# A two-layer hybrid encoder: another order of the instructions, ten weight tiles made by DMA, squares on ScalarE, an output stage in two halves

## The chip, the cores and the metric

The kernel runs on one core of a Trainium2 chip. The metric is the device time of one execution in microseconds (us), the median of several runs. A profiled execution gives the trace from which the rows below come. Engines: PE is TensorE, PEld its weight loads, DVE is VectorE, ACT is ScalarE, POOL is GpSimd, SP is SyncE, which here issues DMAs only.

## What is computed

The reference is an encoder trunk of two layers on 512 tokens of width 1024, all in float32. Per layer:

```python
h = rms_norm(x, g_mix);  z = h @ w_in            # 1024 -> 2560: q, k, v, xb, gb
o = diff_attention(rope(q), rope(k), v, lam)     # 4 heads, two score maps of width 64 each
c = centred_dwconv(xb)                           # width 4
h_f, h_b = rg_lru(c, forward), rg_lru(c, reverse)
r = rms_norm((h_f + h_b) * gelu(gb), lru_norm_g)
x = x + concat(rms_norm(o), r) @ w_out
x = x + cross_attention(rms_norm(x), rms_norm(mem))   # 4 heads, 256 memory tokens
x = x + square(relu(rms_norm(x, g_mlp) @ mlp_w1)) @ mlp_w2   # 4096 hidden
```

and after both layers `rms_norm(x, g_final)`.

## The kernel before

The residual stream lies transposed in SBUF as eight tiles `x[c]` of 128 channels by 512 tokens. Each float32 operand of a large matmul is used as two float32r parts: `hi`, the value as ScalarE converts it on writing a float32r tile, and `lo`, the difference, which VectorE subtracts (`split`). A product is three matmuls: hi by hi, hi by lo and lo by hi, added up in PSUM. The weights lie in memory as 126 tiles of 128 by 1024 a layer. `weight` loads one with a DMA on SP into a `wraw` tile (three buffers), and splits it into `whi` and `wlo` (three buffers each); `gemm_fm` makes from it 24 matmuls of 128x128 by 512 columns. The second MLP product works on pairs of weight tiles: `right_pair` and `left_pair` form sums and differences, and `seven` computes a 2x2 block product by seven half-wide products in place of eight, each of 12 matmuls of 256 columns, and adds them to halves (`LO`, `HI`) of two residual tiles. In `mlp_pair`, a tile of the first MLP product is multiplied by the broadcast norm `rb` and put through max(t, 0) * t, both on VectorE.

A layer has these stages: the v products, a mixing stage (16 units of attention, `FILL` microseconds of other work placed after each, which a generator takes from the letters of `ORDER`: X, Y convolutions, P, R gates, p, r scans, 1 to 3 heads, B and b the gate branch, N its norm, K the keys and values of the memory), the output projection, cross-attention, its projection, and the MLP in four blocks.

The program is first recorded as a list of operations. `Plan.schedule` then places them: each engine takes, of the operations that can begin soonest, the one with the smallest key. A key is the TensorE time recorded before the operation, less a lead in us (`plan.ahead`): `LOAD_AHEAD` for loads, `SPLIT_AHEAD` for splits, `ATT_AHEAD` for attention. `cost` prices each operation, and buffers are counted. A ScalarE operation that needs another function table has `SWITCH` added to its key, and `WAIT` to its start if it would begin late. The resulting order is emitted as the order of each engine's queue; each queue is in order on the chip. All operations are emitted by one line, L414, so a row is told apart by its tile names.

A norm collects squares (`Norm.add`), sums over partitions by matmuls with a column of ones, scales on VectorE, takes the power -1/2 on GpSimd (`rsqrt_small`), and is broadcast by TensorE transposes (`bcast`). At the end eight outputs of 128 by 512 are multiplied with the last broadcast, two on GpSimd and six on VectorE, and stored by SP.

Of the kernel before, what the change touches and what calls it, by code (L numbers as in the profile page):

```python
# [11 lines left out]
F32 = mybir.dt.float32  # L12
# [28 lines left out]
NW = 3  # L41
NSM = 24
NMM = 3
ORDER = ["XYPp1Rr2B3bNK", "XY1Pp2Rr3BbNK"]
FILL = [[8.6, 7.6, 8.6, 7.6, 10.8, 9.7, 11.9, 6.5, 11.9, 7.6, 8.6, 10.8, 7.6, 5.4, 5.4, 7.6],
        [10.8, 7.6, 8.6, 7.6, 8.6, 10.8, 6.5, 10.8, 10.8, 10.8, 7.6, 7.6, 9.7, 3.2, 1.1, 6.5]]
LAG = 2
POOL_OUT = (0, 1)
ATT_AHEAD = 3
SPLIT_AHEAD = 12.0  # L50
LOAD_AHEAD = 65.0


PC = {}
# [96 lines left out]
class Plan:  # L151
# [5 lines left out]
    OWN = {"pe": 0.0, "dve": 0.127, "act": 0.1, "pool": 0.1, "sp": 0.05}  # L157
    LOOK = 0.0
    TABLE = 1.283
    SWITCH = 25.0  # L160
    WAIT = 2.5
    SETS = {"Exp": ("exp",), "Tanh": ("exp", "sig", "gelu"), "Sigmoid": ("sig",), "Sqrt": ("sqrt",),
            "Gelu_apprx_tanh": ("gelu",), "Sin": ("sin",)}

# [30 lines left out]
    def cost(self, eng, m, a, k):  # L195
        out = a[0] if a else k["out"]
        n = 1
        for d in out.shape[1:]:
            n *= d
        if eng == "pe":  # L200
            if m == "transpose":
                return 0.109
            f32 = a[1].root.dtype == F32
            if n < 64:
                return 0.224
            return n * 0.00176 if f32 else max(0.114, n * 0.000456)
        if m == "dma_start":
            return 0.06
        if eng == "act":
            t = 0.093 + n * 0.000833  # L210
            t += 0.093 * sum(isinstance(k.get(x), _View) for x in ("scale", "bias", "accum_out"))
            return t
        if eng == "dve":
            if m == "tensor_reduce":
                n = 512
            if m == "tensor_scalar_mul":
                return 0.066 + n * 0.0007
            ap = m == "scalar_tensor_tensor" and isinstance(a[2], _View)
            return 0.067 + n * 0.00105 + 0.06 * ap
        if eng == "pool" and n <= 4:  # L220
            return 1.0
        if eng == "pool":
            return 0.1 + n * (0.0022 if m != "memset" else 0.001)
        return 0.06

    def record(self, eng, m, a, k):
# [18 lines left out]
        if m == "dma_start":  # L245
            v = out[0] if out else k["in_"]
            op.bytes = 4
            for d in v.shape:
                op.bytes *= d
        if m == "activation":  # L250
            op.table = self.SETS.get(str(a[2]).split(".")[-1])
        for v in allv:
# [18 lines left out]

    def schedule(self):
        ops = self.ops
        for op in ops:
            op.preds.discard(op)
            op.behind -= op.preds | {op}
            op.npred = len(op.preds) + len(op.behind)
            for p in op.preds:
                p.succ[op] = True
            for p in op.behind:  # L280
                p.succ[op] = False
# [34 lines left out]
        def look(e):  # L316
            best, smin, tries = [], 1e18, 0
            for key, idx in cand[e]:
                op = ops[idx]
                st = max(free_at[e], op.ready)  # L320
                ok = True
                need = {}
                for r in op.new:
                    if r.tag in slots:
                        need[r.tag] = need.get(r.tag, 0) + 1
                for tag, n in need.items():
                    fr = sorted(slots[tag])[:n]
                    st = max(st, fr[-1])
                    w, h = waiting[tag], head[tag]
                    while h < len(w) and w[h] in placed:  # L330
                        h += 1
                    head[tag] = h
                    if st >= 1e17:
                        ok = False
                    elif w[h] != idx and n + sum(i > w[h] for i in alive[tag]) > spare[tag]:
                        ok = False
                tries += 1
                if ok:
                    if op.table and table not in op.table:
                        key += self.SWITCH  # L340
                        st += self.WAIT if st > free_at[e] else 0.0
                    best.append((st, key, idx))
                    smin = min(smin, st)
                if tries >= 60 and best:
                    break
            if not best:
                return None
            lim = smin + self.LOOK
            return min(((k, i, s) for s, k, i in best if s <= lim))

        dirty = set(self.engines)
        while left:
# [5 lines left out]
                raise RuntimeError("no instruction can be placed: " + str(  # L358
                    {t: sum(s < 1e17 for s in v) for t, v in slots.items()}))
            e = pick[1]  # L360
            _, idx, st = choice[e]
            op = ops[idx]
            cand[e].remove((op.key, idx))
            dur = op.dur
# [52 lines left out]
def trunk(tc, ctx, xT, memT, pos, W, par, outT):  # L417
# [18 lines left out]
    def T():  # L436
        return plan.tile("b", [P, S], F32)
# [24 lines left out]
    def raw_weight(l, t, ahead=None):  # L462
# [8 lines left out]
                SP.dma_start(out=raw, in_=W[l * NT + t])  # L471
        return raw

    def weight(l, t):
        raw = pre.pop(t, None) if l == 0 else None
        first = raw is not None
        if raw is None:
# [43 lines left out]
    def pc(l, name, i):  # L521
        o = l * NPL + PC[name] + i
        return prm[:, o:o + 1]

    ident = C([P, P], F32, "ident")
    G.memset(ident, 0.0)
# [470 lines left out]
        out[3] = [(dh[:, i * P:(i + 1) * P], dh[:, 512 + i * P:512 + (i + 1) * P]) for i in range(4)]  # L997
        return out

    def seven(l, ta, tb, left, ca, cb, order=range(4)):  # L1000

        w = right_pair(l, ta, tb)
        X, Y, Z = MM(), AT(), AT()
# [15 lines left out]
        add(ca, LO, X, ALU.add)  # L1019
        prod(2, Z, True)  # L1020
        add(ca, LO, Z, ALU.add)
        prod(6, X, False)
        add(cb, LO, X, ALU.subtract)
        prod(5, Y, True)
# [155 lines left out]
    def mlp_pair(l, bk, p, xs, rb):  # L1180

        ts = []
        for i in (2 * p, 2 * p + 1):
            pm = MM()
            gemm_fm(l, T_W1 + 8 * bk + i, xs, pm)
            t = T()
            V.tensor_tensor(t, pm, rb, op=ALU.mult)
            V.scalar_tensor_tensor(t, t, 0.0, t, op0=ALU.max, op1=ALU.mult)
            ts.append(t)
        return left_pair(*ts)  # L1190

# [21 lines left out]
    for l in range(DEPTH):  # L1213
# [64 lines left out]
        def finish(hd, h):  # L1278
# [3 lines left out]
                cat[h] = hd.out()  # L1282
            later(1, out)

        for u in range(16):
            h, qc = divmod(u, 4)
            if qc == 0:
# [50 lines left out]
        for bk in range(4):  # L1338
# [2 lines left out]
                nrm = Norm()  # L1341
                xs = [None] * KD
            for m in range(0, 8, 2):
                seven(l, T_W2 + 8 * bk + m, T_W2 + 8 * bk + m + 1, hid, m, m + 1)
                for c in (m, m + 1) if bk == 3 else ():
                    if l + 1 < DEPTH:
                        xs[c] = prep_x(l + 1, "g_mix", c, nrm)
                    else:
                        nrm.add(x[c])
                        xs[c] = T()  # L1350
                        A.activation(xs[c], x[c], AF.Copy, scale=prm[:, P_FINAL + c:P_FINAL + c + 1])
            if bk < 3:
                nxt += [mlp_pair(l, bk + 1, p, xs, rb) for p in range(1, 4)]
            hid = nxt

    rt = nrm.rstd(D, 4)
    bp = AT()
    bcast(rt, 4, bp)
    rb = plan.tile("rb", [P, S], F32)
    A.activation(rb, bp, AF.Copy)  # L1360
    for c in POOL_OUT + tuple(c for c in range(KD) if c not in POOL_OUT):
        o = T()
        if c in POOL_OUT:
            G.tensor_tensor(o, xs[c], rb, op=ALU.mult)
        else:
            V.tensor_tensor(o, xs[c], bp, op=ALU.mult)
        SP.dma_start(out=outT[c * P:(c + 1) * P, :], in_=o)

    order = plan.schedule()
    plan.emit(tc, order)  # L1370
# [73 lines left out]
```

## Time and profile before

| what | value |
|---|---|
| median of 3 runs | 1506.97 us (1505.68 to 1511.34) |
| the profiled execution's own time | 1508.43 us |
| its span, first to last instruction | 1506.6 us |
| mean granted TensorE clock | 0.984 |
| busy: TensorE, VectorE, ScalarE, GpSimd | 1446.8, 1159.3, 731.7, 26.5 us |
| TensorE matmul instructions | 8038 |
| DMA traffic | 152.43 MB, on average 101 GB/s |
| share of the chain of waits: TensorE, VectorE, ScalarE | 80%, 11%, 4% |

Matmuls are pipelined, and a matmul's busy time overlaps the next one's; so a busy share of TensorE near 100% means that it always had a matmul under way, and not that each took its shortest time. The granted clock of a stretch is a share of 2.4 GHz; a value between 0.5 and 1 is a mean over time at 1.2 and at 2.4 GHz.

### The profile page before, as it was taken

The page shows a single profiled execution, that of the slowest core. Times are in us where ns is not written, and L with a number is a line of the kernel's source. Part 1 is how long each engine was busy: PE and PEld are TensorE (multiplying, and loading weights), DVE is VectorE, ACT ScalarE, POOL GpSimd, SP SyncE. Part 2 cuts the span into 40 slices and gives each one's busy share as a digit, 9 for nine tenths or more (in the row PEclk, how much of TensorE's full clock was granted, in tenths as well). Part 3 has the DMA queues.
Part 4 walks back from the last instruction along what each step waited for, and adds up shares of the span by engine and source line. Part 5 has one row for each costly group of instructions (what it writes and reads, how often), then busy time and mean ns, then how long its engine had stood idle before and what let it go on. Part 6 is the DMA issues. An engine that isn't in the chain of part 4 may idle for free.

```text
span 1506.6 us, 20763 instructions
## 1 busy us (share of the span) xinstructions
PE 1446.8 (96%) x8038; PEld 1239.1 (82%) x8038; DVE 1159.3 (77%) x1959; ACT 731.7 (49%) x1105; POOL 26.5 (2%) x46
## 2 busy tenths in 40 slices
PE   8978999999999999999999989999999999999996
PEld 6756888888888989898887768888888898988985
DVE  7888886555679797887958799855556887969695
ACT  6587765334434343433534887643443433434343
POOL 1000000000000000000000000000000000000000
PEclk9988999999999999999999999999999999999998
DMA  5332442321222222222224444432122223232321
GB/s 198 112 101 71 144 153 92 112 70 43 99 97 93 104 99 98 98 96 101 85 103 121 112 106 149 137 112 83 59 70 84 99 99 112 82 104 89 118 84 58
DMA packets 47666, 152.43 MB, mean 101 GB/s; under 512 B 6096, under 2 KB 6224, under 8 KB 47568
## 3 DMA queue, kind: packets, MB, share of 16 engines
q1 hardware_dynamic: 47424, 150.85, 30.2%
q8 instruction: 63, 1.03, 0.3%
q14 instruction: 35, 0.29, 0.1%
q10 hardware_dynamic: 144, 0.26, 0.1%
HBM read 136.41 MB, written 2.10 MB: 92 GB/s over the span
## 4 chain that ended last, share of the span: by engine, by line
PE 80%; DVE 11%; ACT 4%; issue 2%; DMA 1%; SPq 1%; POOL 0%; DVEq 0%; ACTq 0%; POOLq 0%
PE mm L414 63%; PE at L414 18%; DVE b L414 6%; DVE wlo L414 3%; ACT b L414 3%; DVE pt L414 1%; ACT L414 1%; SPq L414 1%; DMA b<-b 1%; DVE s L414 1%; ACT whi L414 0%; POOL s L414 0%; DVE c_x L414 0%; DMA wraw<-in_memT 0%; DMA c_x<-in_xT 0%
## 5 line engine op out<-in xcount | busy, mean ns | idle before, releaser
L414 PE MATMUL mm<-b,whi 128*128 128x512 f32 (+1 forms) x3648 | 985.5, 358 | 11.7 <-ACT b L414 5.0
L414 PEld LDWEIGHTS mm<-b,whi 128*128 128x128 f32 x3648 | 638.5, 189 | 119.7 <-ACT b L414 6.3
L414 PE MATMUL mm<-b,wlo 128*128 128x512 f32 (+1 forms) x1824 | 650.1, 356 | 10.2 <-DVE wlo L414 10.2
L414 ACT ACTIVATE whi<-wraw 128x1024 fp32r<-128x1024 f32 (+1 forms) x223 | 233.4, 1048 | 357.4 <-issue 155.2
L414 PEld LDWEIGHTS mm<-b,wlo 128*128 128x128 f32 x1824 | 344.5, 189 | 67.4 <-DVE wlo L414 12.6
L414 DVE TENSOR_TENSOR wlo<-wraw,whi 128x1024 fp32r<-128x1024 f32 (+1 forms) x223 | 268.9, 1206 | 40.9 <-ACT whi L414 40.4
L414 DVE TENSOR_TENSOR b<-b,b 128x512 fp32r<-128x512 f32 (+2 forms) x390 | 224.7, 593 | 16.0 <-ACT b L414 14.4
L414 ACT ACTIVATE b<-b 128x256 fp32r<-128x256 f32 (+2 forms) x224 | 130.3, 596 | 150.2 <-DVE b L414 146.7
L414 DVE TENSOR_TENSOR c_x<-c_x,mm 128x256 f32<-128x256 f32 (+1 forms) x160 | 73.7, 471 | 77.8 <-PE mm L414 76.4
L414 ACT ACTIVATE whi<-pt 128x1024 fp32r<-128x1024 f32 x64 | 67.9, 1061 | 101.8 <-PE mm L414 75.7
L414 PE MATMUL at<-b,whi 128*128 128x256 f32 x512 | 92.0, 278 | 0.0
L414 DVE TENSOR_TENSOR b<-mm,rb 128x512 f32<-128x512 f32 x72 | 49.4, 687 | 53.5 <-PE mm L414 53.4
L414 DVE TENSOR_TENSOR wlo<-pt,whi 128x1024 fp32r<-128x1024 f32 x64 | 78.1, 1220 | 0.6 <-ACT whi L414 0.3
L414 ACT ACTIVATE b<-at,s 128x512 f32<-128x512 f32 (+2 forms) x100 | 61.0, 617 | 34.8 <-DVE s L414 34.1
L414 PEld LDWEIGHTS at<-b,whi 128*128 128x128 f32 x512 | 77.7, 188 | 0.0
L414 PE MATMUL at<-b,b 128*128 128x256 f32 (+1 forms) x320 | 67.3, 341 | 5.8 <-DMA b<-b 3.7
L414 DVE TENSOR_REDUCE s<-at 128x1 f32<-128x512 f32 (+1 forms) x80 | 54.3, 686 | 24.0 <-PE at L414 24.0
L414 PE MATMUL at<-b,wlo 128*128 128x256 f32 x256 | 71.2, 278 | 0.0
L414 PEld LDWEIGHTS at<-b,b 128*128 128x128 f32 x320 | 48.2, 196 | 13.6 <-DMA b<-b 4.4
L414 PE MATMUL at<-pt,b 128*128 128x256 f32 (+1 forms) x288 | 51.3, 325 | 4.9 <-ACT pt L414 2.9
L414 DVE TENSOR_TENSOR c_x<-c_x,at 128x256 f32<-128x256 f32 x96 | 40.0, 417 | 18.4 <-PE at L414 17.8
L414 PEld LDWEIGHTS at<-pt,b 128*128 128x128 f32 x288 | 43.8, 192 | 11.5 <-ACT pt L414 3.2
(124 smaller groups left out, 1267.0 us busy)
## 6 DMA issues: line engine op xcount, KB each, us to landing
wraw<-in_W SPq DMA_DIRECT2D x249, 512.0 KB, 3.3
b<-b SPq DMA_DIRECT2D x96, 128.0 KB, 2.3
wraw<-in_memT SPq DMA_DIRECT2D x4, 512.0 KB, 4.3
out_T<-b SPq DMA_DIRECT2D x8, 256.0 KB, 2.6
c_x<-in_xT SPq DMA_DIRECT2D x7, 256.0 KB, 6.1
wraw<-in_W SPq DMA_DIRECT2D x6, 256.0 KB, 4.8
c_x<-in_xT ACTq DMA_DIRECT2D x1, 256.0 KB, 3.2
c_prm<-in_par SPq DMA_DIRECT2D x1, 89.0 KB, 3.0
```

The lines of the kernel that those rows point to most:

```text
L414: getattr(self.engines[op.eng], m)(*a, **k)
```

## The change

A table `LEADS` has one character for each recorded operation; it shifts that operation's key by between -20 and +20 us. The letter L stands for no shift; most operations have another. The mixing stages' `ORDER` and `FILL` are others; loads and splits get longer leads; the planner prices a DMA issue at 0.43 us (0.9 on GpSimd) instead of 0.06, and treats table switches and its sequence of starts a little differently.

Five weight tiles a layer (`DMA_T`: the keys of head 0, the queries of head 2, one tile of the gate branch, one of the memory keys, the last of the memory values) are no longer loaded raw. A GpSimd DMA converts the tile from memory into `whi`; ScalarE writes its negative into `wlo`; a second GpSimd DMA adds the tile from memory to that.

In `mlp_pair` one VectorE operation makes max(pm, 0) * rb, and ScalarE squares it. The last `seven` of the kernel runs its products in another order (`early`), in which three of the four residual halves are done before the last two products, and the last norm and the outputs are made for each half of the tokens by itself: sixteen stores of 128 by 256. There the squares of the last two residual tiles are added by the matmuls with ones instead of by VectorE, and the gain `g_final` is applied by the VectorE multiply, so that ScalarE's scaled copies remain for GpSimd's two tiles only.

```diff
-ORDER = ["XYPp1Rr2B3bNK", "XY1Pp2Rr3BbNK"]
-FILL = [[8.6, 7.6, 8.6, 7.6, 10.8, 9.7, 11.9, 6.5, 11.9, 7.6, 8.6, 10.8, 7.6, 5.4, 5.4, 7.6],
-        [10.8, 7.6, 8.6, 7.6, 8.6, 10.8, 6.5, 10.8, 10.8, 10.8, 7.6, 7.6, 9.7, 3.2, 1.1, 6.5]]
+ORDER = ["XYPp1Rr23BKbN", "XYP1p2Rr3BbNK"]
+FILL = [[14.1, 2.1, 8.6, 0.0, 17.3, 6.7, 6.9, 7.5, 11.9, 7.1, 0.0, 15.3, 13.2, 7.4, 4.4, 15.2],
+        [8.8, 14.6, 8.6, 9.6, 9.1, 7.4, 1.5, 15.3, 15.8, 16.8, 1.8, 1.1, 6.5, 1.5, 3.7, 4.0]]
+PRE = [0.0, 0]
-SPLIT_AHEAD = 12.0
-LOAD_AHEAD = 65.0
+SPLIT_AHEAD = 18.0
+LOAD_AHEAD = 105.0
+CAST_AHEAD = 28.0
+NEG_AHEAD = 20.0
+DMA_T = (1, 4, 13, 36, 51)
+LEAD_STEPS = '#$%&()*+,-./0123456789:;<=>?@ABCDEFGHIJKLMNOPQRSTUVWXYZ[]^_`abcdefghijklmnopqrstu'
+LEADS = (
+    'uL63BCuGGgGGGG@@<<HGuue>d>auFOMu9Q-ZAAGA-2D-H)?NNOC*@%AD?EA#6&/,0,?CBBB,=5>BBDFA?1J1C-G;JF$80?FUFKP;'
...
-    SWITCH = 25.0
-    WAIT = 2.5
+    SWITCH = 52.0
+    WAIT = 3.5
+    HOLD = 0.0
...
         if m == "dma_start":
-            return 0.06
+            return 0.9 if eng == "pool" else 0.43
...
+        for op, c in zip(ops, LEADS):
+            op.key -= LEAD_STEPS.index(c) / 2 - 20.0
...
+    def weight_dma(l, t):
+        hi = plan.tile("whi", [P, 1024], F32R)
+        lo = plan.tile("wlo", [P, 1024], F32R)
+        src = W[l * NT + t]
+        with plan.ahead(CAST_AHEAD):
+            G.dma_start(out=hi, in_=src)
+        with plan.ahead(NEG_AHEAD):
+            A.activation(lo, b(hi), AF.Copy, scale=-1.0)
+            G.dma_start(out=lo, in_=src, accum_op=ALU.add)
+        return hi, lo
+
     def weight(l, t):
+        if t in DMA_T:
+            return weight_dma(l, t)
...
-            V.tensor_tensor(t, pm, rb, op=ALU.mult)
-            V.scalar_tensor_tensor(t, t, 0.0, t, op0=ALU.max, op1=ALU.mult)
+            V.scalar_tensor_tensor(t, pm, 0.0, rb, op0=ALU.max, op1=ALU.mult)
+            A.activation(t, t, AF.Square)
...
+        if early:
+            prod(5, Y, True)
+            add(cb, HI, Y, ALU.add)
+            prod(6, X, False)
+            add(cb, LO, X, ALU.subtract)
+            prod(3, Y, False)
+            add(cb, LO, Y, ALU.add)
+            prod(7, X, False)
+            add(cb, HI, X, ALU.subtract)
+            add(ca, HI, X, ALU.add)
+            prod(4, Z, True)
+            add(ca, HI, Z, ALU.add)
+            return
...
-    rt = nrm.rstd(D, 4)
-    bp = AT()
-    bcast(rt, 4, bp)
-    rb = plan.tile("rb", [P, S], F32)
-    A.activation(rb, bp, AF.Copy)
...
+    outs = [T() for c in range(KD)]
+    for cs in (LO, HI):
+        st = AT()
+        sq = T()
+        for i in range(2):
+            A.activation(sq[:, i * HT:(i + 1) * HT], x[6 + i][:, cs], AF.Square)
+        for c in range(2):
+            with plan.group():
+                for i, q in enumerate((nrm.acc[:, cs], sq[:, :HT], sq[:, HT:])):
+                    PE.matmul(st[:, c:c + 1], q[:, c * P:(c + 1) * P], ones[:, 0:1], start=(i == 0), stop=(i == 2))
+        ms = SM(2)
+        V.tensor_scalar(ms, st[:, :2], 1.0 / D, EPS, op0=ALU.mult, op1=ALU.add)
+        rt = rsqrt_small(ms, 2)
+        bp = AT()
+        bcast(rt, 2, bp)
+        rb = plan.tile("rb", [P, HT], F32)
+        A.activation(rb, bp[:, :HT], AF.Copy)
+        for c in POOL_OUT + tuple(c for c in range(KD) if c not in POOL_OUT):
+            o = outs[c][:, cs]
+            if c in POOL_OUT:
+                G.tensor_tensor(o, xs[c][:, cs], rb, op=ALU.mult)
+            else:
+                V.scalar_tensor_tensor(o, x[c][:, cs], gfin(c), bp[:, :HT], op0=ALU.mult, op1=ALU.mult)
+            SP.dma_start(out=outT[c * P:(c + 1) * P, cs], in_=o)
```

## Rows read from the trace of the kernel before

**Rows 1.** Windows by stage: start:end length, busy us (instructions) by engine, clock, DMA.
```profile
75.00:125.00 50.00, 36.07 (x145) 27.90 (x144) 42.14 (x71) 45.31 (x75) 0.63 (x3) 0.78 0.30 85
175.00:200.00 25.00, 20.99 (x149) 19.37 (x149) 23.53 (x47) 16.31 (x29) 3.19 (x3) 0.93 0.51 147
416.00:760.00 344.00, 337.64 (x2113) 300.43 (x2114) 286.23 (x474) 136.44 (x174) 1.01 (x1) 1.00 0.28 97
830.00:880.00 50.00, 43.41 (x188) 34.55 (x187) 40.52 (x69) 45.40 (x68) 1.01 (x1) 0.90 0.40 108
880.00:950.00 70.00, 66.86 (x422) 58.45 (x421) 67.15 (x116) 51.60 (x87) 2.32 (x2) 1.00 0.44 136
1151.00:1491.20 340.20, 334.82 (x2100) 298.23 (x2099) 280.09 (x466) 135.19 (x172) 1.01 (x1) 1.00 0.26 90
```

**Rows 2.** The chain of waits in order of time: start, us, what.
```profile
256.13 42.00 PE mm L414 x180
...
1483.31 2.83 PE mm L414 x24
```

**Rows 3.** TensorE's instructions by shape, 75 to 125 us: count | busy, mean ns | idle before.
```profile
L414 PE MATMUL mm<-b,whi 128*128 128x512 f32 x56 | 20.1, 442 | 5.6 <-ACT b L414 3.7 <-DVE b L414 1.9
L414 PE MATMUL mm<-b,wlo 128*128 128x512 f32 x29 | 12.6, 435 | 0.0
L414 PE MATMUL at<-b,b 128*128 128x512 f32 x14 | 6.5, 586 | 2.6 <-DMA b<-b 2.4 <-PE at L414 0.2
```

**Rows 4.** TensorE's instructions by shape, 830 to 880 us.
```profile
L414 PE MATMUL mm<-b,whi 128*128 128x512 f32 x83 | 28.6, 427 | 2.2 <-ACT b L414 1.3 <-DVE b L414 0.9
L414 PE MATMUL mm<-b,wlo 128*128 128x512 f32 x41 | 17.0, 414 | 0.0
L414 PE MATMUL at<-b,b 128*128 128x512 f32 x16 | 5.8, 462 | 1.7 <-ACT b L414 1.7
```

**Rows 5.** TensorE's waits, 416 to 760 us: total us, times, longest.
```profile
PE mm L414 <- DVE wlo L414: 4.6, 5, 1.3
```

**Rows 6.** Timeline of VectorE, 462 to 475 us: start, duration, what.
```profile
465.43 0.69 DVE L414 SCALAR_TENSOR_TENSOR b<-b 128x512 f32<-128x512 f32 x1
466.03 0.69 DVE L414 TENSOR_TENSOR pt<-wraw,wraw 128x512 f32<-128x512 f32 x1
...
472.38 1.22 DVE L414 TENSOR_TENSOR wlo<-wraw,whi 128x1024 fp32r<-128x1024 f32 x1
473.52 0.68 DVE L414 TENSOR_TENSOR pt<-pt,wraw 128x512 f32<-128x512 f32 x1
```

**Rows 7.** Timeline of SP's queue, 106 to 112 us: start, length of all, count.
```profile
106.10 4.96 SPq L414 DMA_DIRECT2D b<-b  x8
```

**Rows 8.** DMA issues by kind: count, KB each, median us from issue to landing.
```profile
wraw<-in_W SPq DMA_DIRECT2D x249, 512.0 KB, 3.3
...
c_x<-in_xT SPq DMA_DIRECT2D x7, 256.0 KB, 6.1
```

**Rows 9.** GpSimd's instructions by group, whole span.
```profile
L414 POOL TENSOR_TENSOR s<-s,c_mhalf 128x4 f32<-128x4 f32 (+1 forms) x18 | 21.3, 1182 | 1396.0 <-DVE s L414 1396.0
```

**Rows 10.** VectorE's instructions by shape, whole span.
```profile
L414 DVE SCALAR_TENSOR_TENSOR b<-b 128x512 f32<-128x512 f32 x64 | 44.1, 689 | 1.4
...
L414 DVE SCALAR_TENSOR_TENSOR b<-mm,rb 128x512 f32<-128x512 f32 x16 | 11.1, 691 | 31.5 <-PE mm L414 31.5
```

**Rows 11.** ScalarE's instructions by shape, whole span.
```profile
L414 ACT ACTIVATE b<-b 128x512 f32<-128x512 f32 x48 | 28.4, 622 | 0.2
```

**Rows 12.** The chain of waits in order of time, 1485 us to the end.
```profile
1491.20 0.43 DVE c_x L414
...
1493.05 0.70 DVE b L414
...
1498.03 0.69 DVE b L414
```

**Rows 13.** The stores of the output: duration of one issue in ns, min/median/max.
```profile
L414 SPq DMA_DIRECT2D out_T<-b x8: 332/426/594, 1498.7 to 1502.6; - x8
```

More of the change, by code (lines that the diff above doesn't have):

```diff
@@ L249, in record @@
                 op.bytes *= d
+            if "accum_op" in k:
+                op.bytes *= 2
         if m == "activation":
@@ L273, in schedule @@
         ops = self.ops
+        assert len(ops) == len(LEADS)
+        for op, c in zip(ops, LEADS):
+            op.key -= LEAD_STEPS.index(c) / 2 - 20.0
         for op in ops:
@@ L338, in look @@
                 if ok:
+                    at = st
                     if op.table and table not in op.table:
                         key += self.SWITCH
-                        st += self.WAIT if st > free_at[e] else 0.0
-                    best.append((st, key, idx))
+                        st += self.WAIT if st > free_at[e] else self.HOLD
+                    best.append((st, key, idx, at))
                     smin = min(smin, st)
@@ L348, in look @@
             lim = smin + self.LOOK
-            return min(((k, i, s) for s, k, i in best if s <= lim))
+            return min(((k, i, s, at) for s, k, i, at in best if s <= lim))
         dirty = set(self.engines)
@@ L360, in schedule @@
             e = pick[1]
-            _, idx, st = choice[e]
+            _, idx, _, st = choice[e]
             op = ops[idx]
@@ L523, in pc, with gfin @@
         return prm[:, o:o + 1]
+    def gfin(c):
+        return prm[:, P_FINAL + c:P_FINAL + c + 1]
     ident = C([P, P], F32, "ident")
@@ L998, in right_pair, with seven @@
         return out
-    def seven(l, ta, tb, left, ca, cb, order=range(4)):
+    def seven(l, ta, tb, left, ca, cb, order=range(4), early=False):
         w = right_pair(l, ta, tb)
@@ L1283, in finish @@
             later(1, out)
+        fill(PRE[l])
         for u in range(16):
@@ L1343, in trunk @@
             for m in range(0, 8, 2):
-                seven(l, T_W2 + 8 * bk + m, T_W2 + 8 * bk + m + 1, hid, m, m + 1)
+                end = l + 1 == DEPTH and bk == 3
+                seven(l, T_W2 + 8 * bk + m, T_W2 + 8 * bk + m + 1, hid, m, m + 1, early=end and m == 6)
                 for c in (m, m + 1) if bk == 3 else ():
-                    if l + 1 < DEPTH:
+                    if not end:
                         xs[c] = prep_x(l + 1, "g_mix", c, nrm)
-                    else:
+                    elif m < 6:
                         nrm.add(x[c])
+                    if end and c in POOL_OUT:
                         xs[c] = T()
-                        A.activation(xs[c], x[c], AF.Copy, scale=prm[:, P_FINAL + c:P_FINAL + c + 1])
+                        A.activation(xs[c], x[c], AF.Copy, scale=gfin(c))
             if bk < 3:
@@ L1354, in trunk @@
             hid = nxt
-    rt = nrm.rstd(D, 4)
-    bp = AT()
-    bcast(rt, 4, bp)
-    rb = plan.tile("rb", [P, S], F32)
-    A.activation(rb, bp, AF.Copy)
[L1361 to L1367, printed above, removed]
+    outs = [T() for c in range(KD)]
[22 more added lines that the diff above has]
+            SP.dma_start(out=outT[c * P:(c + 1) * P, cs], in_=o)
     order = plan.schedule()
```

60 lines of the change are left out of this document (added).

## The prediction

> **What bounds the kernel now.** The profile gives TensorE (PE) busy for 96% of the span and most of the chain of waits, so the first question is how much of that is matmul streaming and how much is loss. I read the windows by stage first [rows 1], looking for stretches where PE is busy for less than the stretch or where the granted clock is under 1.00. Two kinds of stage stand out. The out-projection is full (the chain's piece at 256.13 is 42 us of matmuls without a break [rows 2]), as is the cross-attention; the two mixing stages and the two MLPs are not. In 75 to 125 us PE is busy for 36.07 of 50 us at a granted clock of 0.78; in 830 to 880 for 43.41 of 50 at 0.90. The MLPs lose 344 - 337.64 = 6.4 us and 340.2 - 334.82 = 5.4 us, at full clock.
>
> Busy time hides the second loss: after an idle PE the clock falls from 2.4 to 1.2 GHz, and a matmul at the lower one counts as busy for longer. So I price what PE did by its rate where it never waits. The chain of waits has 180 matmuls of 512 columns in 42.00 us and 24 of 256 columns in 2.83 us [rows 2]: 0.233 and 0.118 us each. In 75 to 125 us there are 56 + 29 + 14 = 99 matmuls of 512 columns [rows 3]; the other 145 - 99 = 46 are narrower and are counted at 0.118 at most. That is 23.1 + 5.4 = 28.5 us of streaming in 50: 21.5 lost, 13.9 as idle time and 7.6 to the clock. In 830 to 880, 83 + 41 + 16 = 140 of 512 [rows 4] and 48 narrower ones make 32.6 + 5.7 = 38.3: 11.7 lost, 6.6 idle and 5.1 clock. In 175 to 200 I take 4.0 idle and, at a mean clock of 0.93, half of the 3.5 us at the lower clock: 5.8. In 880 to 950, 3.1 idle. The mixing stages together lose 21.5 + 11.7 + 5.8 + 3.1 = 42 us, the MLPs 11.7, and from the last MLP matmul to the end there are 15 us. That is all this change can reach; the rest is matmul streaming, of which it takes nothing away.
>
> What holds PE in the mixing stages is the other two engines: in 75 to 125 ScalarE is busy for 45.31 and VectorE for 42.14 of 50 us; in 880 to 950 VectorE for 67.15 of 70 [rows 1]. Over both whole stages they are far from full, so a better order has room. In the MLP, PE waits for VectorE's low halves, five times in layer 0 [rows 5].
>
> **The lead table, orders and pacing.** These add and remove nothing; they move work. Their value is the 42 us, and how much is recovered depends on whether the planner's picture fits the chip. Its VectorE cost for 512 elements is 0.067 + 512 x 0.00105 = 0.605 us and for 1024 it is 1.142. The trace's durations are longer (0.69, 1.22), but the starts of back-to-back instructions are 466.03 - 465.43 = 0.60 and 473.52 - 472.38 = 1.14 us apart [rows 6]: the planner prices a full queue rightly. Its price for a DMA issue, 0.06 us before and 0.43 after on SP, comes nearer to the row of eight issues in 4.96 us, 0.62 each [rows 7]. So an order found by the planner should largely hold. From below the value is nothing (stalls move), from above all 42. I take two thirds, 28 us: a part is real shortage of ScalarE and VectorE in the densest stretches, which no order removes.
>
> **Five weight tiles a layer by DMA.** Ten times the kernel drops one SP load, one ScalarE conversion and one VectorE subtraction. It gets instead a converting GpSimd DMA, a ScalarE negating copy of the same shape, and an accumulating GpSimd DMA. VectorE gains 10 x 1.14 = 11.4 us [rows 6], in the stages where it is short; ScalarE breaks even; SP loses ten issues. I put that gain inside the two thirds, since it pays only as a shorter stall. The trace has no DMA issued by GpSimd. For landing, the nearest rows are a plain 512 KB load at 3.3 us and, in the crowd at the start, 6.1 us [rows 8]; even twice the latter is under the lead of 20 us that the accumulation gets, so I cost it at nothing. What hides it is that lead. For the issue, which occupies GpSimd, the bounds are nothing and the 1.18 us of GpSimd's small power operation [rows 9], twenty times; behind it in that queue stand just those powers (18 in all, on the way to every norm's broadcast) and the small memsets. GpSimd works for 26.5 us in the whole span, so the issues alone fit. The tile also holds one of three high buffers for 28 us instead of 12 to 18. PE needs 24 x 0.233 = 5.6 us for a tile, so the other two can still alternate; with no slack there, the loss would be one 2 us split per tile, 20 us in all. I take zero.
>
> The Trainium skill, DMA: Bandwidth & Descriptors, section Anatomy of one DMA, gives for a GpSimd-issued DMA about 2.0 us plus bytes at 436 GB/s, an estimate of 3.2 us for 512 KB; the sum would be the same, and no run here shows it yet.
>
> **Squares on ScalarE.** 64 times a VectorE multiply and a max-multiply (64 in [rows 10]) become one VectorE operation that reads PSUM (nearest row 0.69 us [rows 10], the length of the one that goes), and a square on ScalarE of about 0.62 us [rows 11]. VectorE gains 64 x 0.60 = 38 us of about 566 in the two MLPs; ScalarE gets 40 us more on top of about 272 in 684. PE itself gets nothing from this except where it waited: at most 11.7 us. Ahead of such a wait VectorE works nearly without a gap, and two hidden tiles fall there, one with the max-multiply at 465.43 [rows 6], so 2 x 0.60 = 1.2 us leave the queue ahead of a wait that is at most 1.3 us long [rows 5]. That would clear the low-half waits nearly; the waits at the start of the fourth block may remain, since there the chain from the last hidden tile gets longer by the handover to ScalarE (below 1 us, twice). From both sides: 0 and 11.7; I take 7.
>
> **The tail by halves.** Now the chain from the last residual add at 1491.20 to the first output multiply at 1498.03 takes 6.8 us, and the outputs follow [rows 12]. Eight outputs of 256 KB become sixteen of 128 KB. The low half's chain can start two products, 2 x 12 x 0.118 = 2.8 us, before the last one. It is shorter than now by VectorE's two adds (two of 0.70 [rows 12]) and by half-wide operations; from both sides 4.0 to 6.8 us. The first output is then issued between 1491.2 - 2.8 + 4.0 + 0.5 = 1492.9 and 1495.7. But SP has sixteen issues to make, at 0.62 us each when they follow each other [rows 7]: the last begins 15 x 0.62 = 9.3 us later, at 1502.2 to 1505.0, where it is now 1502.6. If SP keeps up at the 0.43 us median of the outputs now [rows 13], 6.5 us later, the end of VectorE's work decides and about 3 us are gained. So the tail moves by -3 to +2.5 us; I take -0.5.
>
> **Sum.** 28 + 7 + 0.5 = 35.5 us less. The profiled execution took 1508.4 us with a span of 1506.6, within 0.1% of the median 1507.0; from the median, 1507.0 - 35.5 = 1471.5.
>
> **The rivals.**
> Nearly all is recovered: 42 of the mixing stages, 10 of the MLPs, 2 at the end, 54 in all: 1453. For it: planner and chip agree on VectorE's rate, and the clock's part of the loss goes with the idle time by itself. Against it: ScalarE at 45 of 50 us.
> The stalls move and do not shrink: MLP and tail alone pay, 1507.0 - 7.5 = 1499.5. For it: VectorE and ScalarE are near full just where PE idles, and some of the waits there are on ScalarE [rows 3], which the weight change does not relieve. Against it: slack on both sides of these stretches.
> The GpSimd DMAs come late, and the kernel is slower. An accumulation that lands after its 20 us makes PE wait; worse, GpSimd's queue is in order, so a DMA whose negated tile is not ready holds the power behind it, and PE's broadcast waits. In 75 to 125 us 13.9 us of idle time brought 7.6 us of slow clock, about half as much again. Ten tiles late by d us cost 15 d; from d = 2.4 us the whole gain of 35.5 is gone, and at 3.5 us the time is about 1524. Against it: the lead is three times the longest load in [rows 8].
> The Trainium skill, SBUF — State Buffer, section SBUF: two separate sides, adds a mechanism for this rival: GpSimd cannot write descriptors while VectorE runs an operation that takes both ports, so such a DMA looks blocked. It names single-source SBUF copies; nearly all VectorE work here has two tensor sources, and no run shows it yet.
>
> **How the numbers follow.** The forecast (1460 to 1488) 0.57; nearly all recovered (1445 to 1460) 0.16; stalls move (1490 to 1512) 0.15; DMAs late (1515 to 1545) 0.12. Leaving out half of the best case and most of the worst gives 1450 to 1513. A measurement of this kernel tells some 0.5%, 7.5 us, from no change. Faster by more: 0.57 + 0.16 and about a quarter of the third, 0.77. Within it: 0.11. Slower: 0.12.
>
> **What would show it.** Right: in the windows, the mixing stages' PE share near 95% with clock near 1.00 and their end some 18 us earlier in layer 0 and 28 in all by the end of layer 1's; five fewer VectorE subtractions a layer; no idle PE on low halves at the start of an MLP block; sixteen outputs about 0.6 us apart on SP, the span after the last MLP matmul still about 15 us. Wrong: PE waiting for a DMA into a weight tile, or for a GpSimd power that stood behind one; the clock down in other stretches than now; PE waits on ScalarE's squares in the MLP; or issue of the outputs not being what paces the tail.

## The result, and the profile after

The changed kernel takes 1464.45 us (median of 4, 1463.46 to 1467.02) against 1507.05: a ratio of 0.9711, 95% interval [0.9695, 0.9727], or 42.6 us less. The profiled execution took 1463.5 us with a span of 1461.7 us and a mean granted clock of 0.995.

The windows of the changed kernel by stage answer to [rows 1]. The first two stand at the same times as there; the later stages of layer 0 begin some 16 us earlier and those of layer 1 20 to 36 us, and their windows are moved to match:

```profile
75.00:125.00 50.00, 48.00 (x220) 36.94 (x218) 44.27 (x75) 43.79 (x69) 2.12 (x5) 1.00 0.43 114
175.00:200.00 25.00, 25.00 (x196) 23.97 (x195) 23.87 (x40) 17.88 (x30) 0.00 (x0) 1.00 0.49 160
395.00:741.00 346.00, 345.00 (x2162) 307.47 (x2161) 272.79 (x448) 155.72 (x209) 1.01 (x1) 1.00 0.30 98
810.00:860.00 50.00, 47.58 (x226) 38.44 (x225) 48.67 (x87) 46.22 (x76) 2.54 (x3) 1.00 0.57 148
860.00:930.00 70.00, 67.83 (x440) 60.03 (x438) 64.94 (x112) 50.09 (x85) 5.92 (x4) 1.00 0.51 154
1111.00:1449.20 338.20, 337.36 (x2136) 300.98 (x2135) 264.72 (x441) 150.96 (x203) 1.71 (x2) 1.00 0.28 92
```

In 75 to 125 us TensorE now gets through 220 matmuls where it did 145, at a granted clock of 1.00 instead of 0.78, with VectorE and ScalarE about as busy as before. So in this window the other engines are as full as they were, but TensorE's work lies between theirs. In 810 to 860 us VectorE is even busier (48.67 of 50 us where it was 40.52), and TensorE's idle time still falls from 6.6 to 2.4 us. The MLPs have 1.0 and 0.8 us of idle TensorE left of 6.4 and 5.4. Of its waits on low halves in the first MLP one is left, for which [rows 5] had five:

```profile
PE mm L490 <- DVE wlo L490: 0.9, 1, 0.9
```

To compare versions I cut each at the starts of its last residual adds. These are the changed kernel's, from the timeline of VectorE (end of the output projection, cross-attention and MLP of layer 0, then of layer 1 the same):

```profile
277.89 0.69 DVE L490 TENSOR_TENSOR c_x<-c_x,mm 128x512 f32<-128x512 f32 x1 [1.50 <-PE mm L490]
394.88 0.69 DVE L490 TENSOR_TENSOR c_x<-c_x,mm 128x512 f32<-128x512 f32 x1 [2.20 <-PE mm L490]
740.76 0.42 DVE L490 TENSOR_TENSOR c_x<-c_x,mm 128x256 f32<-128x256 f32 x1
993.52 0.69 DVE L490 TENSOR_TENSOR c_x<-c_x,mm 128x512 f32<-128x512 f32 x1 [2.21 <-PE mm L490]
1110.59 0.69 DVE L490 TENSOR_TENSOR c_x<-c_x,mm 128x512 f32<-128x512 f32 x1 [1.50 <-PE mm L490]
1449.18 0.42 DVE L490 TENSOR_TENSOR c_x<-c_x,at 128x256 f32<-128x256 f32 x1 [1.01 <-PE at L490]
```

The differences of such rows give this table (us; cross-attention is 117.0 or 117.1 in all of them and left out; "table" means the lead table with the new orders, pacing and planner settings, unless the text says otherwise). The medians come from several sessions, in which the kernel before had 1507.1 to 1509.2; what is said below against the kernel before uses the one of the same session:

| version | median | mixing 0 | MLP 0 | mixing 1 | MLP 1 | tail |
|---|---|---|---|---|---|---|
| before | 1507.0 | 294.0 | 349.7 | 268.4 | 345.0 | 15.4 |
| after | 1464.5 | 277.9 | 345.9 | 252.8 | 338.6 | 12.5 |
| after, lead table flat | 1491.1 | 283.2 | 350.2 | 262.7 | 345.0 | 14.1 |
| after, no DMA-made tiles | 1467.3 | 277.3 | 346.7 | 255.7 | 338.3 | 12.4 |
| after, squares on VectorE, same order | 1474.5 | 277.7 | 352.8 | 253.1 | 342.4 | 12.5 |
| after, old tail | 1469.7 | 277.1 | 346.3 | 252.4 | 340.5 | 15.6 |
| before, squares alone | 1507.8 | 295.3 | 349.4 | 267.5 | 344.6 | 16.2 |
| before, DMA-made tiles alone | 1489.6 | 281.7 | 349.3 | 261.1 | 344.8 | 15.7 |
| before, tail alone | 1506.1 | 294.7 | 350.0 | 268.3 | 344.7 | 13.9 |
| table alone | 1488.6 | 277.8 | 353.4 | 257.9 | 349.5 | 15.4 |
| tiles alone, VectorE's load put back | 1496.0 | 284.3 | 350.0 | 264.1 | 344.7 | 16.1 |
| before, random shifts | 1535.9 | 306.4 | 354.0 | 273.2 | 350.4 | 16.2 |

Against the kernel before, the mixing stages give 16.1 + 15.6 us, the MLPs 3.8 + 6.4, the tail 2.9: 44.8 of the 44.9 us between the spans. One correction belongs to it: windows cut at these same rows hold 2161 matmuls in the changed kernel's MLP 0 where there were 2143, and 1277 in its mixing 1 where there were 1296. The planner has put some eighteen 512-column matmuls of layer 1 into the MLP of layer 0. At 0.233 us each [rows 2] that is 4.2 us, so the true shares are about 16.1 and 11.4 in the mixing stages and 8.0 and 6.4 in the MLPs. All versions with the lead table have this shift (18 to 20 matmuls), the others at most three of them: before a row with the table is compared with one without it, some 4.5 us of its MLP 0 belong to its mixing 1.

### The profile page after: what moved, and what is told of

Read it like the earlier page. It is cut to its first block, busy times and chain, and to the rows that moved or that the text cites. A ratio compares the mean times of both kernels' runs of the same rounds, so it can differ in the third digit from the quotient of the medians.

```text
span 1461.7 us, 20808 instructions
## 1 busy us (share of the span) xinstructions
PE 1430.8 (98%) x8054; PEld 1228.4 (84%) x8054; DVE 1108.0 (76%) x1891; ACT 758.2 (52%) x1164; POOL 41.5 (3%) x69
## 4 chain that ended last, share of the span: by engine, by line
PE 82%; DVE 10%; DMA 3%; ACT 3%; issue 1%; POOL 0%; SPq 0%; DVEq 0%; ACTq 0%; POOLq 0%
PE mm L490 63%; PE at L490 18%; DVE b L490 6%; DVE wlo L490 2%; ACT b L490 1%; DVE s L490 1%; DMA b<-b 1%; DMA wlo<-in_W 1%; ACT whi L490 1%; DVE pt L490 1%; DMA whi<-in_W 1%; DMA wraw<-in_W 0%; ACT L490 0%; POOL s L490 0%; SPq L490 0%
## 5 line engine op out<-in xcount | busy, mean ns | idle before, releaser
L490 ACT ACTIVATE whi<-wraw 128x1024 fp32r<-128x1024 f32 (+1 forms) x213 | 223.1, 1048 | 346.3 <-PE mm L490 186.8
L490 DVE TENSOR_TENSOR wlo<-wraw,whi 128x1024 fp32r<-128x1024 f32 (+1 forms) x213 | 257.1, 1208 | 41.3 <-ACT whi L490 40.3
L490 DVE TENSOR_TENSOR b<-b,b 128x512 fp32r<-128x512 f32 (+3 forms) x388 | 223.0, 594 | 10.1 <-ACT b L490 8.6
L490 ACT ACTIVATE b<-b 128x512 fp32r<-128x512 f32 (+2 forms) x288 | 168.8, 602 | 80.7 <-DVE b L490 78.0
L490 DVE SCALAR_TENSOR_TENSOR b<-mm,rb 128x512 f32<-128x512 f32 x80 | 55.2, 690 | 106.5 <-PE mm L490 105.7
L490 PE MATMUL at<-b,pt 128*128 128x256 f32 x384 | 53.8, 278 | 0.0
L490 DVE TENSOR_TENSOR c_x<-c_x,at 128x256 f32<-128x256 f32 x97 | 39.5, 417 | 13.9 <-PE at L490 13.4
```

Source lines behind the costliest of these rows:

```text
L490: getattr(self.engines[op.eng], m)(*a, **k)
```

## The experiments

Ratios are to the kernel before, run on the same chip, with 95% intervals.

**The lead table set flat.**

```diff
-            op.key -= LEAD_STEPS.index(c) / 2 - 20.0
+            pass
```

> The changed kernel with every shift of the lead table at zero; orders, pacing, leads, planner prices, DMA-made tiles, squares and tail stay. Theory O (the searched order recovers the mixing stages' stalls): most of their 32 us gain goes, the time is about 1485 to 1495 us, and the loss stands in the two mixing stages as idle PE and a lower granted clock. Rival V (VectorE's relief by the DMA-made tiles does it): the tiles are still there, so at most 8 us are lost, 1465 to 1473.

1491.05 us, ratio 0.9890 [0.9875, 0.9906]: 26.6 us are gone, the size that the order's theory had, but not the place. Of the 27.6 us between the spans the mixing stages lose 15.2 and the MLPs 10.7; with the moved matmuls counted where they belong, it is some 11.5 and 14. 10.8 and 5.7 us of the mixing stages' gain stay without the table; whether the tiles, the new orders or the planner settings keep them, this run doesn't tell. The MLPs are back at 350.2 and 345.0 us although their squares are on ScalarE. This is where they wait, in the timeline of that run (ScalarE and VectorE ahead of one of TensorE's waits):

```profile
460.23 1.06 ACT L490 ACTIVATE whi<-wraw 128x1024 fp32r<-128x1024 f32 x1 [0.59 <-PE at L490]
...
461.21 0.69 DVE L490 TENSOR_TENSOR pt<-pt,wraw 128x512 f32<-128x512 f32 x1
461.81 1.22 DVE L490 TENSOR_TENSOR wlo<-wraw,whi 128x1024 fp32r<-128x1024 f32 x1
...
463.08 0.19 PEld L490 LDWEIGHTS mm<-b,wlo 128*128 128x128 f32 x1 [1.40 <-DVE wlo L490]
463.09 0.39 PE L490 MATMUL mm<-b,wlo 128*128 128x256 f32 x1 [1.20 <-DVE wlo L490]
```

TensorE ends a product and so frees a buffer; ScalarE can begin the next conversion only then (460.23), VectorE subtracts behind three short operations (461.81, 0.5 us after the conversion ended), and TensorE gets the low half at 463.09, 2.9 us after it freed the buffer. What it had to do in between was shorter. Of these 2.9 us VectorE's queue makes 0.5; the rest is a latency around a loop of three engines, which a lighter queue would not shorten.

**The ten weight tiles loaded and split as the others.**

```diff
-DMA_T = (1, 4, 13, 36, 51)
+DMA_T = ()
```

> The changed kernel with the ten DMA-made weight tiles loaded and split as all others; the table and the rest stay (the operations correspond one to one). Theory O: VectorE gets 11 us of work back, of which a part shows: 2 to 6 us slower, 1466 to 1471. Rival V: the mixing gain rests on that relief: 12 us or more slower, 1477 and above. Rival G (the GpSimd DMAs cost more by lateness than they give): faster, below 1463.

1467.25 us, 0.9736 [0.9715, 0.9756]: 2.8 us slower, where 2 to 6 were expected, but the intervals of this run and of the changed kernel overlap. In the traces mixing 1 is 2.9 us longer and mixing 0 is 0.6 us shorter. With the table, the tiles are worth a few us at most.

**The squares back on VectorE, in the same order.** The order of every queue is the changed kernel's; only the square is emitted as a multiply on VectorE.

```diff
+                if m == "activation" and k.get("square"):
+                    m, a, k, eng = "tensor_tensor", (a[0], a[1], a[1]), {"op": ALU.mult}, "dve"
```

> The changed kernel's very order of instructions on every engine, but the 64 squares are multiplies on VectorE in the place in the order where ScalarE had them. If the squares on ScalarE are what cleared the MLP's waits on low halves (theory S): 8 to 15 us slower, all of it in the two MLPs, 1472 to 1480. If the order cleared them (rival O in the MLP): below 3 us slower, under 1468.

1474.45 us, 0.9783 [0.9769, 0.9798]: 10.0 us slower, 6.9 and 3.8 of it in the MLPs. TensorE's waits in MLP 0:

```profile
PE mm L493 <- DVE wlo L493: 3.5, 3, 1.8
PE mm L493 <- DVE c_x L493: 1.1, 3, 0.5
```

The order is the same, so under the searched order the squares are worth 10 us. Idle time makes 6.0 us of the 10.7 us in the MLPs; the rest stands in TensorE's busy time, for the same number of matmuls (why, see the account of the squares below).

**The old tail.** The last products, the norm and the stores of the kernel before in the changed kernel; shifts of the last operations are zero.

```diff
-        for op, c in zip(ops, LEADS):
+        for op, c in zip(ops, LEADS[:5760]):
```

> The changed kernel with the last products in the old order and the last norm and stores in one piece, eight stores of 256 KB. From the traces the tail after the last residual add is 2.9 us shorter by the change: expected 2 to 4 us slower, 1466.5 to 1468.5. If the tail's gain were an accident of the order before it: within 1 us.

1469.68 us, 0.9753 [0.9735, 0.9771]: 5.2 us slower, more than the 2 to 4 expected. Of the 4.2 us between the spans 3.1 lie in the tail and 1.9 in MLP 1, whose last products have another order and, here, no shifts (the other stages are 0.8 us shorter together).

**Squares alone, on the kernel before.**

```diff
-            V.tensor_tensor(t, pm, rb, op=ALU.mult)
-            V.scalar_tensor_tensor(t, t, 0.0, t, op0=ALU.max, op1=ALU.mult)
+            V.scalar_tensor_tensor(t, pm, 0.0, rb, op0=ALU.max, op1=ALU.mult)
+            A.activation(t, t, AF.Square)
```

> The kernel before with the squares alone moved to ScalarE, planned by its own planner. Theory S of the prediction (freed VectorE time clears the low-half waits): the MLPs are shorter by about 7 us, 1498 to 1502. Theory M, formed after the flat-table run, whose MLPs took 350.2 and 345.0 us with the squares on ScalarE against 349.7 and 345.0 before: the wait is a latency (TensorE frees a weight buffer, ScalarE converts, VectorE subtracts), VectorE's total load does not matter, and the squares alone give nothing: 1504 to 1509.

1507.82 us, 0.9993 [0.9984, 1.0002]: nothing. Cut at its residual adds, VectorE is busy for 274.04 us in MLP 0, where it was 290.08, and TensorE's waits there are what they were:

```profile
PE mm L414 <- DVE wlo L414: 5.1, 5, 1.2
PE mm L414 <- DVE c_x L414: 1.2, 1, 1.2
```

Theory S fails here and M's forecast holds: in the order that this planner finds, 16 us of free VectorE time in a stage do not shorten these waits.

**DMA-made tiles alone, on the kernel before.** `weight_dma`, its leads and the two planner prices that it needs are taken over, nothing else; the planner then places all operations anew.

> The kernel before with the ten DMA-made weight tiles alone; the planner knows an accumulating DMA as twice the bytes and its issue as 0.9 us of GpSimd. Theory O (the relief is worth little by itself): within 5 us, 1502 to 1510. Rival V (VectorE's relief clears the mixing stages): 1495 or below. Rival G (late DMAs): above 1512, with waits of TensorE on the DMA into the low tile.

1489.55 us, 0.9873 [0.9859, 0.9886]: 19.5 us faster. Theory O said within 5 us and missed; V said more than 12 and was right here. All of it is in the mixing stages (12.3 + 7.3 us). So the tiles and the table clear largely the same loss: with the moved matmuls counted where they belong, the mixing stages gain 19.6 us by the tiles alone, some 22 by the table alone (below) and 27.5 by both.

**The tail alone, on the kernel before.**

> The kernel before with the tail alone: last products in the new order, norm and stores by halves. If the tail's gain stands by itself: 3 to 5 us faster, 1502 to 1504. If SP's issues eat it, as the prediction had it: within 1 us.

1506.14 us, 0.9985 [0.9976, 0.9994]: 2 to 3 us faster, 1.5 of them in the tail itself. Between the two theories.

**The table alone.** Orders, pacing, planner settings and lead table of the changed kernel without tiles and new tail and with VectorE squares planned as such.

> Orders, pacing, leads, planner settings and lead table of the changed kernel, but no DMA-made tiles, squares on VectorE, the old tail (the table holds for all but the last operations). If the parts add up: 1464.5 + 3 + 10 + 5 = about 1482. If the table is of use only with the operations it was searched with: 1490 and above. If the plan is the whole of the mixing gain: the two mixing stages together still 25 us or more shorter than before.

1488.57 us, 0.9863 [0.9849, 0.9876]: well above the 1482 of parts that add up, just below the 1490 of a table that is of use only with its own operations. As cut, the mixing stages together are 26.7 us shorter, but 19 matmuls have left them (4.4 us), so the plan by itself gives some 22 us there and not the 25 or more that would make it the whole gain. MLP 0 is 3.7 us longer only because it holds 20 more matmuls (4.7 us); MLP 1 has as many as before and is 4.4 us longer. There the table's shifts cost without the squares that they were searched with. A run with the new orders, pacing and planner settings but neither table nor tiles was not made, so the share of the table itself in these 22 us stays open.

**Tiles alone, VectorE's load put back.** The order of the run with the tiles alone, and for each tile a maximum over 1024 elements on VectorE, whose result is not used.

```diff
+                if "accum_op" in k:
+                    src = op.load.real().bitcast(F32)
+                    self.engines["dve"].tensor_reduce(self.sink.real(), src, axis=AX.X, op=ALU.max)
```

> The kernel before with the ten DMA-made tiles, in exactly the order of that run, and ten maxima over 1024 elements added on VectorE (one per tile, 1.1 us each, results unused, beside the accumulating DMA): VectorE's load is as before, the order and the tiles are not. If VectorE's relief made the 19.5 us (theory V for the kernel before): back by 10 us or more, 1499 or above. If it was another order that came with the replanning (rival): at most 4 us slower, below 1494.

1495.96 us, 0.9917 [0.9903, 0.9931]: between the two. Of 19.6 us in the mixing stages 14.0 stay with VectorE's load as before, so its relief is worth at most some 5.5 us: one of the ten maxima also stopped VectorE for 7.0 us, waiting for its converting DMA. The larger part comes with the order that was planned around the tiles, or with the tile's own path, which no longer stands in VectorE's queue. These two weren't separated and stay open.

**Random shifts.** Each key of the kernel before is shifted by up to 1 us either way.

```diff
+        for op in ops:
+            op.key += rng.uniform(-1.0, 1.0)
```

> The kernel before with an unsearched table: each operation's key shifted at random by up to 1 us either way. If the planner's outcome is a draw that any small change rerolls by 10 us or more, the time is well off 1507 to either side, mostly in the mixing stages; if small shifts average out, 1502 to 1513. Theory O needs a searched table: no gain above 10 us.

1535.93 us, 1.0177 [1.0163, 1.0191]: 26.7 us slower, so the first branch holds, small shifts do not average out; 12.4 and 4.8 us of it are in the mixing stages, 4.3 and 5.4 in the MLPs. Of these two windows in layer 0's mixing stage the first is much as in [rows 1], the second is new; the line below them is the second window in the kernel before:

```profile
75.00:125.00 50.00, 36.03 (x151) 27.92 (x149) 41.67 (x69) 42.77 (x72) 0.13 (x2) 0.83 0.30 85
...
175.00:225.00 50.00, 38.80 (x265) 36.08 (x264) 38.87 (x74) 26.43 (x47) 3.15 (x3) 0.83 0.46 137
...
175.00:225.00 50.00, 45.99 (x321) 42.38 (x321) 44.92 (x80) 31.14 (x54) 3.19 (x3) 0.97 0.50 158
```

This one random table of at most 1 us loses as much as the flat-table run loses against the searched one, so it is not having a table that gains. It is a single draw: how far such draws scatter, and how lucky the order of the kernel before is among them, was not measured.

**The high half's stores on two queues.**

```diff
-            SP.dma_start(out=outT[c * P:(c + 1) * P, cs], in_=o)
+            (A if cs is HI and c % 2 else SP).dma_start(out=outT[c * P:(c + 1) * P, cs], in_=o)
```

> The changed kernel with four of the high half's eight stores issued by ScalarE. If SP's issues, one after another, pace the end (last VectorE multiply ends at 1457.3, last issue at 1458.7): 1 to 1.5 us faster, 1463. If the stores' bandwidth or landing paces it: same, 1464.5.

1463.10 us, 0.9697 [0.9683, 0.9710]. The tail in its trace is 11.9 us against 12.5, half of what was expected: the last issue begins 8.3 us after the last residual add instead of 9.5, but the stores then land up to 2.5 us after their issues, where 1.9 was the most. The interval overlaps the changed kernel's, so the time alone doesn't tell the two apart.

**The same with a lead for the high half's power.**

```diff
+        with plan.ahead(20.0 if cs is HI else 0.0):
```

> As the run before, and the high half's mean and power get a lead of 20 us, so that VectorE's small operation no longer stands behind the low half's multiplies (it began at 1452.6, some 1.2 us after its matmuls). If the high half's chain is what sets the end once the stores have two queues: 2 to 2.5 us faster than the changed kernel, 1462. If not: as the run before.

1464.67 us, 0.9700 [0.9687, 0.9713], tail 11.9 us. VectorE's small operation still began behind the low half's multiplies (1454.8, 3.4 us after the last add, as before the edit), and TensorE, VectorE and ScalarE execute the same operations in the same order as in the run before: the lead moved nothing on them. Presumably the planner believes that the matmuls ahead of it end later than they do; that was not looked into. So the high half's chain wasn't tried, and the 1.6 us between the two medians are not the edit's.

## Why the prediction was right, and where not

The forecast was 1471.5 us; measured 1464.5. Against the sum of 35.5 us the stages gave 44.8: the mixing stages 0.5 us less than their term, the MLPs 7.4 and the tail 2.4 us more. By its steps:

**The mixing stages: 28 us forecast, about 27.5 measured** (31.7 by stage, less the 4.2 us of matmuls that moved into MLP 0), split 16 and 11 where 18 and 10 were forecast. Counting matmuls at the rate of a stretch without waits, and calling the rest loss, gave a ceiling of 42 us that was not reached; 14.2 and 5.0 us of idle TensorE are left in the two stages. The two thirds were a judgement that no row gave, so the close hit is partly luck. No run tested the planner's VectorE prices by themselves. The clock followed by itself: the share granted in 75 to 125 us went from 0.78 to 1.00 once the idle time was gone, as the prediction's sum had it.

**The tiles inside that sum.** Leaving them without a term of their own was right for this sum (2.8 us on top of the table, within the noise), but for a wrong reason: they are worth 19.5 us where the table isn't there, and at most about 5.5 of it is VectorE's relief, the one effect that the prediction named. Costing the DMAs at nothing held but for 1.6 us. The profile's part on DMAs:

```profile
wraw<-in_W SPq DMA_DIRECT2D x239, 512.0 KB, 3.3
b<-b SPq DMA_DIRECT2D x96, 128.0 KB, 2.5
whi<-in_W POOLq DMA_DIRECT2D x10, 512.0 KB, 4.0
wlo<-in_W POOLq DMA_DIRECT2D x10, 512.0 KB, 5.5
```

The converting DMA lands after 4.0 us at the median (7.6 at most) and the accumulating one after 5.5 (7.2 at most), against the prediction's rows of 3.3 and 6.1. The estimate by the Trainium skill (DMA: Bandwidth & Descriptors, Anatomy of one DMA), 2.0 us plus the bytes at 436 GB/s, was 3.2 us for 512 KB; the trace has 0.8 us more for the converting and 2.3 us more for the accumulating DMA. The rival of late DMAs happened once, for 1.6 us (TensorE's waits, 200 to 243 us):

```profile
PE mm L490 <- DMA wlo<-in_W: 1.6, 1, 1.6
```

And GpSimd was occupied (ns, min/median/max) for

```profile
L490 POOL DMA_DIRECT2D wlo<-in_W x10: 857/869/925, 32.0 to 941.2; - x10
```

below the 1.18 us taken as the upper end, and nearly the same in all ten. Of the mechanism in the Trainium skill's SBUF — State Buffer (SBUF: two separate sides), descriptors held up by VectorE, nothing is to be seen in these issues: VectorE was idle for nearly all of the one at 90.05 us, which took 0.86 us, and busy throughout the one at 873.82, which took 0.86 us too. The worse form of that rival, a power held behind a DMA whose negated tile is not ready, did not happen. The accumulating DMAs did wait at the head of GpSimd's queue,

```profile
POOL wlo L490 <- ACT wlo L490: 45.3, 9, 8.5
```

but no power followed one of them without a pause of GpSimd.

**Squares: 7 us forecast, 10 measured with the table (same order), 0 without it; the MLPs in all 14.4.** The mechanism failed. The step was "two hidden tiles fall there, ... so 2 x 0.60 = 1.2 us leave the queue ahead of a wait that is at most 1.3 us long. That would clear the low-half waits nearly". The squares alone cleared none. In the wait that was followed up (the flat table's) most of the time is the way from a freed buffer over ScalarE and VectorE; what covers it is TensorE having other work meanwhile. The prediction also gave the table nothing in the MLPs ("Their value is the 42 us" of the mixing stages), and there it is worth 10.7 us, or 14 with the moved matmuls. The timeline of TensorE in the changed kernel, at the start of an MLP block:

```profile
446.18 0.39 PE L490 MATMUL mm<-b,wlo 128*128 128x512 f32 x1
446.41 0.40 PE L490 MATMUL mm<-b,whi 128*128 128x256 f32 x2
446.65 0.28 PE L490 MATMUL mm<-b,wlo 128*128 128x256 f32 x1
446.76 0.62 PE L490 MATMUL mm<-b,whi 128*128 128x512 f32 x2
447.23 0.39 PE L490 MATMUL mm<-b,wlo 128*128 128x512 f32 x1
```

Three matmuls of the second MLP product stand among the 512-column ones of the next block, and more follow. That interleaving is the table's: counted in the traces, TensorE changes between 512 and 256 columns 44 times in the first MLP with the table, with the squares or without, and 16 times in the kernel before and with the table flat. But it needs the squares off VectorE: in the same order with the squares back, the waits on low halves return (3.5 us). MLPs together, with the moved matmuls taken off: 694.7 us before, 694.0 with the squares alone, 698 with the table alone, 680 with both.

The price of the waits was too small as well. The prediction capped the MLPs' gain by their 11.7 us of idle time, and they gave 14.4, of which idle time shows 9.9. In the rows above a 256-column matmul counts as busy for 0.28 us, but the next one starts 0.11 us after it; so up to 0.16 us of a late start is hidden in busy time. Counted in the traces from start to start (what goes beyond 0.118 us), the late starts behind 256-column matmuls come to 10.4 + 8.9 us in the two MLPs of the kernel before and to 2.5 + 3.1 in the changed one: 13.7 us less. The same count gives 10.2 + 9.4 with the squares alone, 10.1 + 14.5 with the table alone, and 8.5 + 6.7 with the squares put back in the changed order: neither part clears the waits without the other. What is left is mostly pace: 24 matmuls of 256 columns take 2.83 us [rows 2] or 2.72, as in this row of the changed kernel's chain of waits. More of them take the shorter time in this trace, but that varies without any change of order (last section).

```profile
1272.22 2.72 PE at L490 x24
```

**The tail: 0.5 us forecast, 2.9 measured.** Two terms were mis-sized: when the first output is issued, and the landing of the last store, which had no term. The low half's last add and its first output multiply, in the timeline of VectorE, and the sixteen stores, with the landing of the stores before and after:

```profile
1445.42 0.42 DVE L490 TENSOR_TENSOR c_x<-c_x,at 128x256 f32<-128x256 f32 x1 [0.20 <-PE at L490]
...
1449.54 0.48 DVE L490 SCALAR_TENSOR_TENSOR b<-c_x,c_prm,at 128x256 f32<-128x256 f32 x1
...
L490 SPq DMA_DIRECT2D out_T<-b x16: 333/398/453, 1450.0 to 1458.7; - x16
...
out_T<-b SPq DMA_DIRECT2D x8, 256.0 KB, 2.6
out_T<-b SPq DMA_DIRECT2D x16, 128.0 KB, 1.8
```

The low half starts 3.8 us ahead of the last residual add (1449.18), not 2.8, since its sums are taken between the last products, and needs 4.1 us, near the lower end of the 4.0 to 6.8. So the first store is issued 0.9 us after that add, where the prediction had 1.7 to 4.5. SP's issues then follow 0.58 us apart on average, close to the 0.62 taken, and the last begins 9.5 us after the add instead of 11.4: 1.9 us gained. The other 1.0 us is that the program ends 3.0 us after that issue instead of 4.0, with a store of half the size. SP's queue paces part of the end: with two queues the tail is 0.6 us shorter in both runs. The high half's chain may be the next limit, which is argued and not shown; this is its stretch in the chain of waits:

```profile
1450.66 2.05 DVE b L490 x5
1452.71 0.08 DVE s L490
...
1452.86 0.70 POOL s L490
...
1454.83 0.48 DVE b L490
```

VectorE's mean of the high half stood behind five multiplies of the low half, and began 1.0 us after its matmuls. A half-size tail shares its engines with the other half.

**The rivals.** "Nearly all is recovered" (1453) would have needed the last 14.5 us of the mixing stages' 42. "The stalls move" did not happen, but without the searched table the order gives little: the new orders and pacing with the tiles are no better in the mixing stages (545.9 us) than the old ones with the tiles (542.8).

## What to carry to other kernels

When the bound engine is 96% busy, count its instructions at the rate of a stretch without waits; idle time plus slow clock gives a first estimate of what a reordering can reach. Here two thirds of it came in the mixing stages, and more than all of it in the MLPs, because a late start of a pipelined matmul shows only in part as idle time: count from start to start. Before crediting an edit that unloads an engine, ask whether the wait that it is meant to clear is a backlog or a latency: following one wait back to the moment when its buffer came free tells it, and a lighter queue alone did nothing for the latency here. Parts that clear the same loss don't add, and parts that need each other show nothing alone, so an ablation in one direction misleads: do each part alone, and take each away. When stages are cut at fixed events, count the instructions in each: work that moved across a cut looks like a gain on one side and a loss on the other.

## What was not expected of the hardware

One random shift of the planner's keys by at most 1 us cost 26.7 us. A reading that is not shown: queues that are each in order and wait on each other pass a small change of order on. Where a new idle stretch appeared, the granted clock fell with it (175 to 225 us: 11.2 us idle at 0.83, where it was 4.0 us at 0.97).

Matmuls of 256 columns stream at two paces, 24 in 2.72 or in 2.83 us, at the same granted clock of 1.00, and both kernels show both. The order does not choose between them: in the first MLP, four traces with the same order of instructions there (the changed kernel, its version with the old tail and the two with two store queues) have 547 to 1099 of some 1340 at the faster pace. What chooses was not tried.

A converting and an accumulating DMA of 512 KB occupy GpSimd for 0.57 and 0.87 us at the median and land after 4.0 and 5.5 us, where the plain load takes 3.3.
